# Block products over twenty k tiles of the second FFN projection, with the weights' block sums formed in HBM

## The chip, the cores and the metric

The kernel runs on one core of a Trainium2 chip. The metric is device time in microseconds (us) of one execution. The engines are PE (TensorE, matrix products), DVE (VectorE), ACT (ScalarE), POOL (GpSimd) and SP (SyncE), which here only issues DMAs. Each engine runs its own queue of instructions in order and waits at the head of it on semaphores. DMAs are issued on SP's, ACT's or POOL's queue and are carried out by 16 DMA engines.

## The reference, cut to what matters

One decoder block on x (512 tokens by 1024 channels), fp32. The part that changes is the end of it:

```
h2 = rms_norm(x, norm2_g) * (1 + scale2) + shift2
f_g, f_u = split(h2 @ w_ffn_in)            # w_ffn_in: 1024 x 5632, so two halves of 2816
x = x + gate2 * ((silu(f_g) * f_u) @ w_ffn_out)   # w_ffn_out: 2816 x 1024
return rms_norm(x, final_norm_g)
```

2816 is 22 k tiles of 128 rows. The second FFN projection is therefore a product of 512 tokens, 22 k tiles and 1024 columns.

## The kernel before, in words

Every fp32 product is done in three matmuls. Each operand is split into a rounded high part (an ACT copy to fp32r) and the low rest (a DVE subtraction), and `mm3` (lines 51 to 55) issues high by high, high by low and low by high into the same PSUM bank. A matmul takes 128 rows of k, 128 tokens and up to 512 columns.

The program is written in the order in which it runs on each engine; the semaphores follow from the tiles that the instructions read and write. The buffers are named by tags, and a tag with one buffer is handed on when the last reader of its old tile is done.

Weights come through a stream (lines 58 to 148). `issue` starts the DMA of a chunk of 128 x 1024 elements, 512 KB, into one of three `raw` buffers; `prep` makes its high and low parts in one of three `hi` and three `lo` buffers; `get(i)` makes sure that everything up to two chunks behind chunk i has been prepared and that as many more have been issued as `raw` buffers allow.

The first FFN projection (from line 1620) runs in 20 rounds, q = -2 to 17. A round computes 256 columns of f_g or f_u for all tokens by seven block products (Strassen and Winograd's scheme over halves of tokens, k and columns) of 12 matmuls of 256 columns each. `s_issue(q + 2)` at the head of a round issues two loads of 512 KB on SP's queue; `s_prep(q + 1)` spreads the splits and sums of the next round's weights over the round. In rounds 1 to 8 the last adaLN section is accumulated too (`last_mod`, line 1452 on). The results are the tiles `gq`, 22 of them with 512 tokens each, made by `gtile`.

The second FFN projection follows (lines 1716 to 1859). k tiles 12 to 19 (`KZ`) are done by seven block products, `zprod`, over halves of the tokens (256), of these k tiles (4) and of the columns (512). The sums of activations (`a_sum`) and the differences of weights (`w_sub`) are made by DVE in place, and their splits by `a_hi`, `a_lo`, `w_hi` and `w_lo`. The other 14 k tiles (`KC`) are done plainly, in seven chunks of two k tiles for each of the two column halves (`W_FO`), with the activations split by `g_split` into the tiles `gs`. Behind the first column half stand the residual additions for it (`resid`, line 1162: a product with the gate, an addition to x, and a square with a sum) and `scale_g`, which multiplies by the gain of the final norm. In the second half the last three chunks are done token tile by token tile, so that a row block can be normalised (`row_rstd`, `finish`) while the next one is computed. The last token tile is done in two parts of 256 columns.

The lines that set the two sets of k tiles are these:

```
KZ, KC = (list(range(12, 16)), list(range(16, 20))), list(range(12)) + [20, 21]
W_FO = [[add_w(w_ffn_out, KC[k:k + 2], 512 * h, 512) for k in range(0, len(KC), 2)] for h in range(2)]
```

Of the kernel before, what the change touches and what calls it, by code (L numbers as in the profile page):

```python
# [28 lines left out]
def block_kernel(ctx: ExitStack, tc: tile.TileContext, x, positions, w_ada, b_ada, w_in,  # L29
# [239 lines left out]
    KZ, KC = (list(range(12, 16)), list(range(16, 20))), list(range(12)) + [20, 21]  # L269
    W_FO = [[add_w(w_ffn_out, KC[k:k + 2], 512 * h, 512) for k in range(0, len(KC), 2)] for h in range(2)]  # L270
# [95 lines left out]
    def sec_tasks(flush=False, one=False):  # L366
        tick[0] += 1
        while sec_done:
# [31 lines left out]
    hT = [(base.tile([128, S], F32R, name=f"h{kt}", tag=f"S1_{kt}", bufs=1),  # L400
           base.tile([128, S], F32R, name=f"hl{kt}", tag=f"S1_{8 + kt}", bufs=1)) for kt in range(8)]
# [682 lines left out]
    mT, om, ow, oraw = {}, {}, {}, {}  # L1084
    OM = {"A11": 0, "S1": 1, "S2": 2, "A12": 3, "S3": 0, "S4": 1, "A22": 2}
# [24 lines left out]
    def o_m(key):  # L1110
        om[key] = tuple(base.tile([128, 2, 256], F32R, name="om", tag=f"S1_{OM[key] + 8 * e}", bufs=1) for e in range(2))
        split(*om[key], m_block(key))
# [8 lines left out]
    def pb_evac(g):  # L1121
        def ev(pb):
            for m in range(2):
                k = 2 * g + m
                t, o = t512("mg"), part[k // 4][:, k % 4]
                V.tensor_mul(t, pb[m], gbt[g][:, m])
                V.tensor_add(o, o, t)
                if k >= 4:
                    mT[k] = tuple(base.tile([128, S], F32R, name="mt", tag=f"S1_{k + 8 * e}", bufs=1) for e in range(2))
                    A.activation(mT[k][0], o, AF.Copy)  # L1130
            for k in range(2 * g, 2 * g + 2):
                if k >= 4:
                    V.tensor_sub(mT[k][1], part[1][:, k % 4], f(mT[k][0]))
        return ev
# [27 lines left out]
    def resid(p, c0, n, slot, tk, gate):  # L1162
# [4 lines left out]
        A.activation(t[:, :n], xt[tk][:, cs_], AF.Square, scale=1.0 / 32, accum_out=ss2[:, tk, slot:slot + 1])  # L1167
# [19 lines left out]
    def norm2_T(half):  # L1187

        for kh in range(2):
# [5 lines left out]
            else:  # L1195
                h2f["t", kh, 1] = [base.tile([128, 2, 256], F32, name="h2f", tag=f"S1_{kh * 2 + q}", bufs=1)
                                   for q in range(2)]
# [20 lines left out]
    sraw, sw = {}, {}  # L1218
# [27 lines left out]
    def s_prep(q):  # L1246
# [4 lines left out]
        d = sw[q] = {}  # L1251
        A11, A21, A12, A22 = ra[:, :, 0], ra[:, :, 1], rb[:, :, 0], rb[:, :, 1]

        def a0():
            d["A"] = tuple(base.tile([128, 4, 128], F32R, name="sa", tag="acc", bufs=2) if q == -2 else
                           base.tile([128, 4, 128], F32R, name="sa", tag=f"S1_{4 + 2 * (q % 2) + e}", bufs=1)
                           for e in range(2))
# [149 lines left out]
    gq, gz = {}, []  # L1407

    def gtile(m):
        if m not in gq:  # L1410
            if m < 12:
                gq[m] = base.tile([128, S], F32, name="gq", tag=f"S1_{m + 8 if m < 8 else m - 8}", bufs=1)
            else:
                n = 4 if m < 20 else 2
                t = ffn[0].tile([128, n, S], F32, name="gq", tag=("E5", "E6", "F1")[(m - 12) // 4], bufs=1)
                for e in range(n):
                    gq[m + e] = t[:, e]
                gz.append(t)
# [46 lines left out]
    def last_gate():  # L1465
        t = ffn[0].tile([128, 4, S], F32R, name="ahl", tag="E6", bufs=1)
        for half in range(2):
# [6 lines left out]
    gT = {}  # L1474

    GHOME = ["E1", None, "E3", None, "E0", None, ("S1_4", "S1_5"), ("S1_6", "S1_7"), "S2_2", "S2_3", "E7", None,
             "S2_4", "S2_5"]
    spare = []

    def g_home(n):  # L1480
        h = GHOME[n]
        if h is None:
            return spare.pop()
        if isinstance(h, tuple):
            return [base.tile([128, S], F32R, name="gs", tag=t, bufs=1) for t in h]
        if h[0] == "S":
            t = base.tile([128, 2, S], F32R, name="gs", tag=h, bufs=1)
        else:
            t = ffn[0].tile([128, 4, S], F32R, name="gs", tag=h, bufs=1)
            spare.append((t[:, 2], t[:, 3]))  # L1490
        return t[:, 0], t[:, 1]

    def g_split(upto):
        while len(gT) < min(upto, len(KC)):
            m = KC[len(gT)]
            hi, lo = g_home(len(gT))
            split(hi, lo, gq[m])
            gT[m] = (hi, lo)


    zr, zw, za = {}, {}, {}
    ZW = {"T1": ("E2", "E4"), "T2": ("E1", "E3"), "T3": ("E0", "E7"), "T4": ("E2", "E4"), "B22": ("E1", "E3")}
    ZA = {"A11": 0, "S1": 4, "S2": 6, "A12": 0, "S3": 4, "S4": 6, "A22": 0}

    def z_issue(name):
        kh, h = {"B11": (0, 0), "B12": (0, 1), "B21": (1, 0), "B22": (1, 1)}[name]
        for c in range(2):
            if name == "B11" or name == "B12" and c == 0:
                t = base.tile([128, 2, S], F32, name="raw", tag="raw", bufs=RAWB)
                ts = [t]  # L1510
            elif name == "B12":
                ts = [ffn[0].tile([128, 2, S], F32, name="zraw", tag="F0", bufs=1)]
            elif name == "B22":
                ts = [base.tile([128, 2, S], F32, name="zraw", tag=f"S2_{2 + c}", bufs=1)]
            else:
                ts = [base.tile([128, 1, S], F32, name="zraw", tag=f"S1_{4 + 2 * c + e}", bufs=1) for e in range(2)]
            k = KZ[kh][2 * c]
            for t in ts:
                n = t.shape[1]
                SY.dma_start(t, w_ffn_out[k * 128:(k + n) * 128, h * 512:h * 512 + 512].rearrange("(j p) n -> p j n", p=128))  # L1520
                k += n
            zr[name, c] = ts

    def z_parts(ts, *others):
        o = 0
        for t in ts:
            n = t.shape[1]
            yield (t,) + tuple(x_[:, o:o + n] for x_ in others)
            o += n

    def w_hi(key, c, src):
        if key in ZW:
            t = ffn[0].tile([128, 2, 2, S], F32R, name="zw", tag=ZW[key][c], bufs=1)
            zw[key, c] = (t[:, 0], t[:, 1])
        else:
            zw[key, c] = tuple(base.tile([128, 2, S], F32R, name=n, tag=n, bufs=3) for n in ("hi", "lo"))
        for t, hi in z_parts(zr[src, c], zw[key, c][0]):
            A.activation(hi, t, AF.Copy)

    def w_lo(key, c, src):  # L1540
        for t, hi, lo in z_parts(zr[src, c], *zw[key, c]):
            V.tensor_sub(lo, t, f(hi))

    def w_sub(o, a, b, c):

        (o_,), (b_,) = zr[o, c], zr[b, c]
        for a_, ob, bb in z_parts(zr[a, c], o_, b_):
            V.tensor_sub(ob, a_, bb)

    def a_block(name):  # L1550
        kh, th = {"A11": (0, 0), "A21": (0, 1), "A12": (1, 0), "A22": (1, 1)}[name]
        return gz[kh][:, :, th * 256:(th + 1) * 256]


    AT_ = {"A11": "A11", "A12": "A12", "A22": "A22", "S1": "A21", "S4": "A21", "S2": "A11", "S3": "A11"}

    def a_hi(key):
# [344 lines left out]
```

## Time and profile before

| what | value |
|---|---|
| time, median of 3 runs | 829.84 us (829.57 to 829.93) |
| time of the profiled execution | 829.8 us |
| its span in the trace | 828.0 us |
| PE busy | 815.7 us, 99% |
| DVE busy | 672.2 us, 81% |
| ACT busy | 413.6 us, 50% |
| POOL busy | 108.5 us, 13% |
| bytes moved by DMA | 109.10 MB |
| granted PE clock | 0.998 |

Times inside the trace are counted from the start of the span. Busy times of matmuls overlap, since the array is pipelined: a row's mean duration is longer than the distance between two matmuls, and the distance is what counts for the time. DVE's and ACT's durations contain a short overlap of the same kind. A DMA's "landing" is the time from its issue to its completion.

### The profile page before, as it was taken

The numbers are of one execution on the slowest core, as the hardware profiler recorded it, in microseconds if no ns is written. First come the engines' busy times: TensorE is split into PE (matmuls) and PEld (weight loads), VectorE is DVE, ScalarE is ACT, GpSimd is POOL, SyncE is SP. The second block draws the span as 40 slices with busy tenths as digits, with TensorE's granted clock in tenths as the row PEclk, the third lists the DMA queues.
The fourth block names the chain that finished last, engine by engine and source line by source line (L and its number), as shares of the span: only waits on it lengthen the run. The fifth ranks groups of instructions, "written<-read, shape, count | busy, mean of one in ns | idle before, by whom it ended". The sixth has DMA issues, their size and how long they took to land.

```text
span 828.0 us, 12858 instructions
## 1 busy us (share of the span) xinstructions
PE 815.7 (99%) x4980; PEld 730.0 (88%) x4980; DVE 672.2 (81%) x1161; ACT 413.6 (50%) x722; POOL 108.5 (13%) x101
## 2 busy tenths in 40 slices
PE   7999999999999999999999999999999999999996
PEld 6889889988888888988888899999999999888885
DVE  7989788798899558886697969799998888984635
ACT  5674544323322236665536586555555555563322
POOL 2060032362353411000000000000000000000001
PEclk9999999999999999999999999999999999999999
DMA  9974352423445562057631403445533335143212
GB/s 299 311 201 118 102 178 78 121 85 101 124 136 180 195 181 74 26 158 231 197 102 47 157 27 128 124 152 159 168 111 103 103 102 155 50 153 102 77 51 103
DMA packets 95677, 109.10 MB, mean 132 GB/s; under 512 B 5616, under 2 KB 76272, under 8 KB 95616
## 3 DMA queue, kind: packets, MB, share of 16 engines
q1 hardware_dynamic: 92512, 101.37, 40.2%
q0 software_dynamic: 2384, 6.10, 2.3%
q8 instruction: 39, 0.64, 0.3%
q10 hardware_dynamic: 720, 0.82, 0.3%
q14 instruction: 22, 0.18, 0.1%
HBM read 105.90 MB, written 2.10 MB: 130 GB/s over the span
## 4 chain that ended last, share of the span: by engine, by line
PE 96%; DMA 1%; DVE 1%; issue 0%; SPq 0%; ACT 0%; POOLq 0%; POOL 0%; DVEq 0%
PE pb L55 9%; PE pb L53 9%; PE pb L54 9%; PE R L53 8%; PE R L54 8%; PE R L55 8%; PE pfo L55 5%; PE pfo L53 5%; PE pfo L54 5%; PE pav L54 2%; PE pav L53 2%; PE pav L55 2%; PE pgb L53 2%; PE pgb L54 2%; PE pgb L55 2%; PE po L54 2%
## 5 line engine op out<-in xcount | busy, mean ns | idle before, releaser
L112 ACT ACTIVATE hi<-raw 128x1024 fp32r<-128x1024 f32 (+2 forms) x80 | 82.5, 1034 | 105.4 <-PE pb L54 39.9
L116 POOL TENSOR_TENSOR lo<-raw,hi 128x1024 fp32r<-128x1024 f32 x29 | 73.0, 2522 | 127.8 <-ACT hi L112 122.1
L116 DVE TENSOR_TENSOR lo<-raw,hi 128x1024 fp32r<-128x1024 f32 (+2 forms) x44 | 53.0, 1210 | 41.4 <-ACT hi L112 41.2
L53 PE MATMUL pb<-h,hi 128*128 128x512 f32 (+1 forms) x192 | 74.6, 388 | 0.0
L55 PE MATMUL pb<-h,lo 128*128 128x512 f32 (+1 forms) x192 | 73.9, 385 | 0.0
L54 PE MATMUL pb<-hl,hi 128*128 128x512 f32 (+1 forms) x192 | 73.9, 385 | 0.0
L177 DVE SCALAR_TENSOR_TENSOR acc<-mraw,cols,acc 128x512 f32<-128x512 f32 x49 | 40.1, 818 | 17.9 <-DMA mraw<-in_w_ada_dram 16.9
L55 PE MATMUL pfo<-hi,gs 128*128 128x512 f32 (+1 forms) x126 | 46.4, 369 | 0.0
L54 PE MATMUL pfo<-lo,gs 128*128 128x512 f32 (+1 forms) x126 | 46.4, 368 | 0.0
L53 PE MATMUL pfo<-hi,gs 128*128 128x512 f32 (+1 forms) x126 | 46.4, 368 | 0.0
L53 PE MATMUL R<-tb,sx 128*128 128x256 f32 x160 | 45.2, 282 | 0.0
L54 PE MATMUL R<-tb,sx 128*128 128x256 f32 x160 | 45.1, 282 | 0.0
L55 PE MATMUL R<-tb,sx 128*128 128x256 f32 x160 | 45.0, 281 | 0.0
L55 PE MATMUL R<-tb,lo 128*128 128x256 f32 x160 | 44.8, 280 | 0.0
L53 PE MATMUL R<-tb,hi 128*128 128x256 f32 x160 | 44.8, 280 | 0.0
L54 PE MATMUL R<-tb,hi 128*128 128x256 f32 x160 | 44.6, 279 | 0.0
L55 PEld LDWEIGHTS pb<-h,lo 128*128 128x128 f32 x192 | 36.0, 187 | 7.3
L54 PEld LDWEIGHTS pb<-hl,hi 128*128 128x128 f32 x192 | 36.0, 188 | 6.9
L53 PEld LDWEIGHTS pb<-h,hi 128*128 128x128 f32 x192 | 36.0, 188 | 6.9
L54 PE MATMUL pav<-lo,h 128*128 128x256 f32 x128 | 35.8, 279 | 0.0
L53 PE MATMUL pav<-hi,h 128*128 128x256 f32 x128 | 35.7, 279 | 0.0
L55 PE MATMUL pav<-hi,hl 128*128 128x256 f32 x128 | 35.7, 279 | 0.0
(392 smaller groups left out, 2655.4 us busy)
## 6 DMA issues: line engine op xcount, KB each, us to landing
raw<-in_w_ffn_in_dram SPq DMA_DIRECT2D x44, 512.0 KB, 4.6
raw<-in_w_in_dram SPq DMA_DIRECT2D x40, 512.0 KB, 3.9
mraw<-in_w_ada_dram SPq DMA_DIRECT2D x28, 512.0 KB, 4.1
raw<-in_w_ffn_out_dram SPq DMA_DIRECT2D x17, 512.0 KB, 3.8
s<-in_w_ada_dram SPq DMA_DIRECT2D x30, 256.0 KB, 5.6
raw<-in_w_proj_a_dram SPq DMA_DIRECT2D x8, 512.0 KB, 4.8
raw<-in_w_proj_b_dram SPq DMA_DIRECT2D x8, 512.0 KB, 4.6
raw<-in_w_in_dram SPq DMA_DIRECT2D x9, 256.0 KB, 4.7
```

Of the source, the lines that this page charges most:

```text
L53: T.matmul(o, wh, rh, start=start, stop=False, **kw)
L54: T.matmul(o, wh, rlo, start=False, stop=False, **kw)
L55: T.matmul(o, wlo, rh, start=False, stop=stop, **kw)
L112: A.activation(hi[:, :m], e["raw"][:, :m], AF.Copy)
L116: e["lo"].tensor_sub(lo[:, :m], e["raw"][:, :m], f(hi[:, :m]))
L177: V.scalar_tensor_tensor(o, w, cs[:, j:j + 1], o, op0=OP.mult, op1=OP.add)
```

## The change

- `KZ` becomes 20 k tiles: ten for each half, the k tiles 0 to 19. A block product is then 5 chunks of two k tiles (`NZ = 5`) for 2 token tiles. Only k tiles 20 and 21 are left in `KC`, one chunk for each column half.
- The four sums of weight blocks that the scheme needs are no longer made by DVE from loaded blocks. Four tensors `wsum` of 1280 x 512 elements lie in HBM. `wsum_steps` fills them, in pieces of 256 rows (512 KB): a copy from HBM to HBM on SP's queue, and additions by accumulating DMAs on POOL's queue. With the halves of k and of columns as indices the sums are: 1 is B00 + B01, 3 is B01 + B11, 2 is 1 + B11, 4 is 2 + B10. For each of the five pieces this is four copies and four accumulating DMAs, in six steps. `wstep()` is called twice in each round of the first projection, and takes one step each time.
- Signs are turned so that only additions are needed in HBM: `z_copy` gets a factor of -1 and `z_add` an operation.
- All block operands of weights, those in HBM too, now come through the stream: `zprod` fetches its five chunks by `get` and between them runs a list of small tasks: `a_hi`, `a_lo`, `a_sum` for later products, and residual additions.
- The products are in another order: those that finish column half 0 and parts of half 1, then the plain chunks, then two block products (`"A22"` with sum 4, and `"S4"` with block (1, 1)), between whose chunks the residual additions stand. The three last chunks of the last product are done token tile by token tile.
- `S1` is summed in three parts, in rounds 9, 13 and 16. The 16 tags `S1_0` to `S1_15` of 128 x 512 become four tags `SW0` to `SW3` of 128 x 4 x 512, so that the `gq` tiles lie by fours.

```diff
-    KZ, KC = (list(range(12, 16)), list(range(16, 20))), list(range(12)) + [20, 21]
-    W_FO = [[add_w(w_ffn_out, KC[k:k + 2], 512 * h, 512) for k in range(0, len(KC), 2)] for h in range(2)]
+    KZ = ([0, 1, 2, 3, 4, 5, 6, 7, 12, 13], [8, 9, 10, 11, 16, 17, 18, 19, 14, 15])
+    KC = [20, 21]
+    NZ = 5
+    dram = ctx.enter_context(tc.tile_pool(name="dram", bufs=1, space=bass.MemoryType.DRAM))
+    wsum = {n: dram.tile([NZ * 256, 512], F32, name=f"wsum{n}") for n in (1, 2, 3, 4)}
+    W_Z = {}
...
+    for key in ((0, 0), 1, 2, (1, 0), 3):
+        add_z(key)
+    W_FO = [add_w(w_ffn_out, KC, 512 * h, 512) for h in range(2)]
+    for key in (4, (1, 1)):
+        add_z(key)
+    def wsum_steps():
+        def step(c, *moves):
+            o = slice(256 * c, 256 * c + 256)
+            def fn():
+                for n, add, src in moves:
+                    if isinstance(src, tuple):
+                        k = KZ[src[0]][2 * c] * 128
+                        src = w_ffn_out[k:k + 256, 512 * src[1]:512 * src[1] + 512]
+                    else:
+                        src = wsum[src][o]
+                    if add:
+                        P.dma_start(wsum[n][o], src, accum_op=OP.add)
+                    else:
+                        SY.dma_start(wsum[n][o], src)
+            return fn
+        parts = [[step(c, *m) for m in (
+            ((1, 0, (0, 0)), (3, 0, (0, 1))), ((1, 1, (0, 1)), (3, 1, (1, 1))), ((2, 0, 1),), ((2, 1, (1, 1)),),
+            ((4, 0, 2),), ((4, 1, (1, 0)),))] for c in range(NZ)]
+        return ([fn for c in (0, 2) for two in zip(parts[c], parts[c + 1]) for fn in two] +
+                [fn for one in parts[4] for fn in (one, None)])
...
+    def sw(k, dt, name):
+        return base.tile([128, 4, S], dt, name=name, tag=f"SW{k}", bufs=1)
...
     def z_first():
+        def b(k):
+            return lambda: ensure(wseq[wseq.index(W_Z[0, 0][0]) + k])
+        st["limit"] = 1 << 30
+        return [(b(0), lambda: a_hi("A11", 0), lambda: a_lo("A11", 0)),
+                (b(1), lambda: a_hi("A11", 1), lambda: a_lo("A11", 1)),
+                (lambda: a_hi("A11", 2), lambda: (a_lo("A11", 2), a_sum("S2", 0))),
+                (b(2), lambda: None)]
...
         sprod(R[1], S2_, TB[2], False)
+        wstep()
         A.activation(R[2], R[1], AF.Copy)
...
-        if q == NQ - 2:
-            a_sum("S1")
-    z_issue("B22")
+        wstep()
+        if q in (9, 13, NQ - 2):
+            a_sum("S1", {9: 0, 13: 2}.get(q, 1))
...
+    def zprod(k, ka, kw, start, tasks):
         if start:
             Z[k] = [bank(ZB[k][e], "pfo") for e in range(2)]
+        for c, i in enumerate(W_Z[kw][:len(tasks)]):
+            w = get(i)
+            for fn in tasks[c]:
+                fn()
             for e in range(2):
+                zmm(Z[k][e], ka, c, e, w, ALL, start and c == 0, c == NZ - 1)
...
+    z_copy(1, 0, -1.0)
+    zprod(3, "S1", 1, True, [[lo_("S2", 1), hi_("S2", 2), sm_("S4", 0), lo_("S2", 2)], [sm_("S4", 1), hi_("A12", 0)],
+                             [sm_("S4", 2), lo_("A12", 0)], [hi_("A12", 1)],
+                             [lo_("A12", 1), hi_("A12", 2)]])
...
+    zprod(2, "A22", 4, False, [[res_(0, 0)], [sq_, res_(1, 0)], [sq_, res_(2, 1)], [sq_, res_(3, 1)], [sq_]])
...
+    zprod(1, "S4", (1, 1), False, [[res_(2, 0)], [sq_, res_(3, 0)]])
+    last = bank(7, "pfo")
+    A.activation(last[:, :256], Z[1][1][:, 256:], AF.Copy)
+    ids = W_Z[1, 1][2:]
+    ch = [get(i, 2 - k) for k, i in enumerate(ids)]
+    sq_()
+    done(2)
+    done(3)
+    for tk in range(2):
+        for z in range(2) if tk else (None,):
+            c = ALL if z is None else slice(256 * z, 256 * z + 256)
+            o = Z[1][0] if z is None else (Z[1][1][:, :256], last[:, :256])[z]
+            for n_, w in enumerate(ch):
+                zmm(o, "S4", 2 + n_, tk, w, c, False, n_ == 2)
...
```

384 lines of the change are left out of this document (153 added, 231 removed).

## The prediction

> **What bounds the kernel now.** I read the page first: busy shares, then the chain that ended last.
>
> ```profile
> span 828.0 us, 12858 instructions
> PE 815.7 (99%) x4980; PEld 730.0 (88%) x4980; DVE 672.2 (81%) x1161; ACT 413.6 (50%) x722; POOL 108.5 (13%) x101
> ...
> PE 96%; DMA 1%; DVE 1%; issue 0%; SPq 0%; ACT 0%; POOLq 0%; POOL 0%; DVEq 0%
> ```
>
> The reader is to see 96% of the chain on PE. So matmuls that go away shorten the time, unless their place is taken by a wait. Next come the two stages that the change touches, by their tiles: `R` is the first FFN projection, `pfo` the second. The rows give durations, the first and last start, and the forms.
>
> ```profile
> L53 PE MATMUL R<-h,sa x80: 276/279/289, 503.8 to 695.0; 128*128 128x256 f32 x80
> L55 PE MATMUL R<-tb,sx x160: 277/283/283, 515.4 to 703.9; 128*128 128x256 f32 x160
> ...
> L53 PE MATMUL pfo<-hi,gs x126: 277/392/403, 743.0 to 820.6; 128*128 128x512 f32 x98, 128*128 128x256 f32 x28
> L53 PE MATMUL pfo<-zw,za x40: 389/394/400, 709.6 to 742.4; 128*128 128x512 f32 x40
> L53 PE MATMUL pfo<-hi,za x16: 392/396/400, 704.0 to 725.7; 128*128 128x512 f32 x16
> ...
> L55 PE MATMUL pfo<-hi,gs x126: 278/392/398, 743.5 to 820.8; 128*128 128x512 f32 x98, 128*128 128x256 f32 x28
> ```
>
> Each product is three such lines (L53, L54, L55). `R`: 20 rounds of 84 matmuls, 503.8 to 703.9, hence 0.119 us for 256 columns and 10.0 us a round. `pfo`: (98+40+16) x 3 = 462 matmuls of 512 columns and 28 x 3 = 84 of 256, from 704.0 to 820.8. With 84 x 0.119 = 10.0 us for the narrow ones, 462 share 106.8 us: 0.231 us each. Neither stage leaves PE idle, and the stages join without a gap.
>
> **The change part by part.** *Matmuls.* Before: 7 products x 4 k tiles x 2 token tiles x 3 = 168, and 14 x 4 x 2 x 3 = 336; in all 504 widths of 512. After: 7 x 10 x 2 x 3 = 420 and 2 x 4 x 2 x 3 = 48; in all 468. Only the last 18 widths are cut in two, so 450 wide and 36 narrow ones remain. Saved: 12 x 0.231 + 48 x 0.119 = 2.8 + 5.7 = **8.5 us**, all of it on the path.
>
> *DVE and ACT in the second projection.* A chunk now feeds 12 matmuls, 2.77 us, where a plain chunk fed 24. Its splits, and the distance of DVE operations of that size:
>
> ```profile
> L112 ACT ACTIVATE hi<-raw 128x1024 fp32r<-128x1024 f32 x14 | 14.7, 1058 | 39.2 <-PE pfo L55 35.3 <-DMA raw<-in_w_ffn_out_dram 3.8
> ...
> 724.73 1.21 DVE L1542 TENSOR_TENSOR zw<-raw,zw 128x1024 fp32r<-128x1024 f32 x1
> 725.86 1.21 DVE L1542 TENSOR_TENSOR zw<-zraw,zw 128x1024 fp32r<-128x1024 f32 x1
> ...
> 704.00:743.00 39.00, 39.00 (x170) 31.54 (x169) 35.86 (x42) 24.59 (x32) 0.53 (x1) 1.00 0.29 95
> ```
>
> DVE starts one every 1.13 us. A product lasts 60 x 0.231 = 13.9 us and asks DVE for five weight splits (5.7) and at most six operations on activations (6.8): 12.5 us at most, in the product with `S1`. ACT has five splits and at most about five other copies, some 10 us. DVE was busy 35.86 of 39 us while PE never paused, so I cost this at 0. The weight differences and the `gs` splits that go away were under PE too: also 0. `S1`'s sums in rounds 9 and 13 (1.13 and about 0.6 us) stand beside a PE that has 10 us of work a round; DVE has room there (third row of windows below): 0. The four wide tags are handed on at points where all readers of the old tile are a stage back: 0. By my reading the third chunk of the first product is asked for twice in round 17, by the stream's own rule and explicitly: 512 KB more under a full PE, 0.
>
> *Loads of the second projection.* 512 KB per 2.77 us is 189 GB/s.
>
> ```profile
> raw<-in_w_ffn_out_dram SPq DMA_DIRECT2D x17, 512.0 KB, 3.8
> raw<-in_w_ffn_in_dram SPq DMA_DIRECT2D x44, 512.0 KB, 4.6
> ...
> L1233 SPq DMA_DIRECT2D raw<-in_w_ffn_in_dram x40: 367/368/501, 460.0 to 674.0; - x40
> ...
> DMA to landing us min/median/max: 3.4/4.6/7.0
> ```
>
> With three `raw` buffers, one goes around in issue 0.4 + landing 3.8 + `hi` 1.06 + `lo` 1.21 = 6.5 us, and PE needs it every 8.3 us; prepared chunks are two ahead. I cost this at 0, with little room: landings of 5.6 us would use it up.
>
> *HBM sums in the first projection.* 20 copies on SP's queue and 20 accumulating DMAs on POOL's, 512 KB each, in rounds -2 to 15. POOL has no other work here, so what its DMAs wait for delays only them. SP's queue is shared: a copy of step 3 or 5 waits for accumulations of the step before, and behind it stand the next rounds' loads, for which ACT waits, and with it PE. The 16 engines' share and rate in the three stretches of six rounds:
>
> ```profile
> 507.00:566.00 59.00, 59.00 (x499) 59.00 (x499) 51.08 (x70) 33.42 (x60) 0.00 (x0) 1.00 0.45 138
> 566.00:625.00 59.00, 59.00 (x500) 59.00 (x499) 55.95 (x78) 34.41 (x62) 0.00 (x0) 1.00 0.46 141
> 625.00:684.00 59.00, 59.00 (x496) 58.82 (x496) 49.60 (x67) 33.62 (x60) 0.00 (x0) 1.00 0.34 101
> ...
> 561.67 12.55 SPq L1233 DMA_DIRECT2D raw<-in_w_ffn_in_dram  x4
> ...
> 574.85 0.62 ACT L1258 ACTIVATE sa<-raw 128x512 fp32r<-128x512 f32 x1
> ```
>
> 141 GB/s at 0.46 is 307 GB/s for all engines, so 512 KB costs 1.71 us of them. That is my price of a copy. No row shows an accumulating DMA. Bounds: below, a plain transfer's 1.71 us; above, the longest landing of 512 KB on POOL's queue, taken as if nothing overlapped:
>
> ```profile
> xr<-in_x_dram POOLq DMA_DIRECT2D x4, 512.0 KB, 4.3
> ...
> gate1b<-in_b_ada_dram POOLq DMA_DIRECT2D x1, 512.0 KB, 9.3
> ```
>
> I take 2.6 us: a copy reads and writes each byte once, an accumulation reads two operands and writes one, so three streams for two; landings contain a wait for completion that others can use, so the lower end is nearer. The first two stretches each take two of the five pieces: 0.45 x 59 = 27 us of loads, eight copies 13.7, eight accumulations 20.8, together 61 of 59 us. The third takes one piece: 20 + 6.8 + 10.4 = 37 us. What spills over is made good there. A load issued at 561.67 was first read at 574.85, 13.2 us later, and lands in 4.6: 8.6 us of slack. Dependent steps stand two rounds (20 us) apart in a stretch. So SP may stand for some microseconds without PE noticing, and the price is 0; if the slack is used up, every further microsecond is PE's.
>
> The Trainium skill, "DMA: Bandwidth & Descriptors", section "Issuing engines are not separate DMA queues", says that DMAs of all issuing engines run on the same 16 engines and interleave. By it the idle POOL gives no capacity of its own, as assumed above; without it the accumulations would cost nothing at any price. No run here shows either yet.
>
> *The tail.* In the last product DVE has chunk splits, two residuals (three operations of 128x512 each, 0.62 us apart) and two row ends, all on one queue:
>
> ```profile
> 744.08 1.29 DVE L306 TENSOR_TENSOR gs<-gq,gs 128x512 fp32r<-128x512 f32 x2
> ```
>
> Counting from that product's start: the split of its third chunk ends at 2.5 us (its `hi` buffer comes free at 0), residual 4.4, split 5.5, residual 7.4, split of the last chunk 8.5. PE wants that at 5.5 + 2.8 = 8.3: 0.3 us lost. The row ends and a third residual keep DVE until about 0.3 us after the last matmul's result. Before, DVE had idled 0.64 us when that result came:
>
> ```profile
> 821.14 0.42 DVE L1165 TENSOR_TENSOR rt<-pfo,gate2b 128x256 f32<-128x256 f32 x1 [0.64 <-PE pfo L55]
> ...
> 823.53 0.61 ACT L1708 ACTIVATE xo<-xo,sm 128x384 f32<-128x384 f32 x1 [0.96 <-POOL sm L1171]
> ```
>
> The 7 us from 821.14 to the span's end are the same work in both. Bounds of this term: 0 and, if a whole residual stands in front, 2; I take **+0.6**.
>
> Sum: 829.8 (span 828.0 and 1.8 around it) - 8.5 + 0.6 = **821.9 us**. The profiled execution is 0.04 us under the median 829.84, which changes nothing.
>
> **The rivals.**
>
> *The sums in HBM hold SP (slower).* Place: the copies of sums 2 and 4 on SP's queue, with the loads behind them. Over 177 us the engines have 74 us of loads (0.45, 0.46 and 0.34 of 59) and 34 of copies; the 20 accumulations, at a us each, fit with the 8.6 us of slack if 108 + 20 a < 185.6, so a < 3.9 us. At a = 4.3 the lost time, about 8 us, eats the gain. At 5 it is 21 us: 843; at 9.3 it would be 107 us: 929. For it speak the load share, already 0.46, and 9.3 in the row above; against it the 4.3 of the `xr` row, a landing with its fixed part.
>
> *The same, partly.* a between 3.9 and 4.2, or bursts in the first stretch alone: 1 to 7 us lost, 823 to 829.
>
> *Loads bound the second projection.* Its share of DMA was only 0.29, but landings rise with traffic (7.0 us at worst in the row above). At 6.2 us a buffer goes around in 8.9 us, 0.2 us per chunk too long: 35 x 0.2 = 7 us, so 829, and slower above that. Against it: nothing else loads then, and 3.8 us is the median of that same stage.
>
> The page cited above gives 341 GB/s for a 1 MB load, in its section "Measured". By that figure a rough estimate of the point at which the first rival eats the gain rises by a tenth or two; the trace shows 307 at these sizes, and I stay with that.
>
> **How the numbers follow.** Forecast 0.50; sums in HBM hold SP, slower 0.22; partly 0.16; loads bound the second projection 0.12. The likeliest case alone spans 820.8 (8.5 saved, 0.5 better at the tail) to 823.5 (2 us at the tail). The range must leave out no more than 2 in 10: 820.5 to 834, which takes in the two middle cases and the mild end of the first rival, and leaves out the rest of that. 0.2% (1.7 us) is about what a measurement can tell from no change. Faster: 0.50 + 0.15 + 0.04 = 0.69; same 0.01 + 0.03 = 0.04; slower 0.22 + 0.05 = 0.27.
>
> **What would show it.** Right: `pfo` rows with 450 wide and 36 narrow matmuls over some 108.5 us; `R` still over 200 us; SP waits at the HBM copies short; DMA share of the first two stretches near 1 at most. An accumulation's own cost shows in the packets and share of the software queue. Wrong by the first rival: ACT at `sa<-raw` waiting for `raw` and `R` longer than 200 us. Wrong by the last: `hi<-raw` in `pfo` waiting for DMA, and PE below 90% there. The tail term is read from the distance between the last matmul and DVE's `rt`.

## The result, and the profile after

| | before | after |
|---|---|---|
| time, median of 6 runs each | 829.88 us | 832.63 us (831.31 to 833.28) |
| ratio, 95% interval | | 1.003 (1.0017 to 1.0043) |
| span of the profiled execution | 828.0 us | 829.5 us |
| first projection (`R`), first start to last start | 200.1 us | 206.2 us |
| second projection (`pfo`), the same | 116.8 us | 109.6 us |
| last issue of ACT's queue ends, to the span's end | 3.5 us | 4.8 us |

The change makes the kernel slower by 0.3%, where 1% faster was forecast. The profiled execution after is the fastest of its runs, so its 1.5 us over before is less than the median's 2.75. It divides so: `R` starts 0.8 later (its start lies between 503.1 and 505.0 in all runs below, with sums and without, so that is no part of the change), `R` +6.1, `pfo` -7.2, and the end behind the last matmul +1.8.

The page after: span, busy shares, the DMA share in 40 slices, and the two queues that carry nearly all bytes (packets, MB, share of 16 engines).

```profile
span 829.5 us, 12872 instructions
PE 810.3 (98%) x4920; PEld 723.6 (87%) x4920; DVE 684.5 (83%) x1167; ACT 427.0 (51%) x730; POOL 126.7 (15%) x121
DMA  9974352423345652057531409899998863556533
q1 hardware_dynamic: 99872, 120.24, 45.7%
q0 software_dynamic: 7824, 16.59, 10.4%
```

The same two queues before:

```profile
q1 hardware_dynamic: 92512, 101.37, 40.2%
q0 software_dynamic: 2384, 6.10, 2.3%
```

DMA now stands at 8 and 9 tenths for eight slices (the 25th on, from 498 us), nearly all of them in the first projection, where before only its loads ran and it stood at 3 to 5. The 20 accumulations are the software queue's 10.49 MB more; they cost 8.1% of 829.5 us, 67 us of all 16 engines, **3.36 us each**. The copies are priced in the first experiment. Such a price is the time of the packets, added up and divided by 16. The share of DMA in the windows below reaches 1.28, so packets' times can overlap in an engine, and a price is not time in which nothing else moves.

The groups by tile: duration, first and last start, forms.

```profile
L53 PE MATMUL R<-h,sa x80: 276/281/289, 504.6 to 701.6; 128*128 128x256 f32 x80
L55 PE MATMUL R<-tb,sx x160: 277/282/283, 516.2 to 710.8; 128*128 128x256 f32 x160
...
L55 PE MATMUL pfo<-hi,za x146: 280/395/397, 711.4 to 820.5; 128*128 128x512 f32 x134, 128*128 128x256 f32 x12
L53 PE MATMUL pfo<-hi,gs x16: 395/396/397, 780.5 to 791.6; 128*128 128x512 f32 x16
```

(134 + 16) x 3 = 450 wide and 36 narrow matmuls, as counted; the second projection starts at 710.9, 6.9 us later than before. Where `R` lost its time is seen in windows of it (PE, PEld, DVE, ACT, POOL busy; granted clock; DMA share; GB/s):

```profile
563.80:583.80 20.00, 20.00 (x171) 20.00 (x171) 19.08 (x27) 10.70 (x19) 3.53 (x4) 1.00 1.01 279
583.80:603.80 20.00, 16.31 (x123) 15.61 (x122) 13.43 (x22) 8.03 (x16) 1.76 (x2) 0.91 0.94 247
...
593.00:595.00 2.00, 2.00 (x14) 2.00 (x13) 1.96 (x3) 0.00 (x0) 0.00 (x0) 0.63 1.28 449
595.00:597.00 2.00, 1.58 (x8) 1.28 (x7) 2.00 (x3) 1.27 (x3) 0.00 (x0) 0.52 1.06 438
```

There is one disturbed place. PE stands for 3.7 of the 20 us from 583.8, and behind its first pause the granted clock is 0.63 and 0.52 for two windows of 2 us, which costs some 0.37 x 2.0 + 0.48 x 1.58 = 1.5 us more. Together that is 5.2 of the 6.1 us; 0.3 of the rest is there without any sums too (first experiment), and 0.6 I can't assign.

Who waits at this place (us in total, times, longest), and the landing of the 40 loads of the first projection:

```profile
DVE acc L175 <- DMA mraw<-in_w_ada_dram: 6.4, 1, 6.4
...
ACT sx L1335 <- DMA raw<-in_w_ffn_in_dram: 3.1, 1, 3.1
...
ACT sa L1324 <- DMA raw<-in_w_ffn_in_dram: 2.1, 1, 2.1
PE R L53 <- ACT R L1670: 2.1, 1, 2.1
```

```profile
DMA to landing us min/median/max: 3.4/6.6/16.1
```

ACT and DVE wait for loads, and PE for ACT. A load of the projection landed after 16.1 us at worst, 7.0 before. In the prediction's rows a load is first read 13.2 us after its issue (4.6 of landing and 8.6 of slack), so 16.1 us is 2.9 too late, and ACT's longest wait for a load is 3.1. What was in the engines is told by the view of DMA from 572 to 584 us, first after, then before:

```profile
q0 software_dynamic: 595, 1.16, 60.3%
q1 hardware_dynamic: 1088, 1.41, 37.8%
```

```profile
q1 hardware_dynamic: 1919, 2.42, 65.8%
```

Four accumulations were issued in these 12 us (572.97, 574.58, 575.88 and 577.18). They took 60.3% of the engines' time, and the loads, together with the last of the copies, got 37.8%, where 65.8% had been the loads': 1088 packets for 1919. That is how the loss in `R` comes about, as far as this trace shows it.

Four accumulations alone are not enough: the first four, issued at 506.75 to 510.74, stopped PE nowhere. The next loads were issued behind them, at 512.79 and after, and landed in 11.3 and 12.2 us, while two loads were issued in the midst of the later four (from 573.48). Nor did SP stand at its copies: its waits name no copy anywhere in this trace, and 71.0 and 50.6 us, the longest of the first projection, are for DVE to free the buffers of the loads.

SP's issues slowed, though: the loads' line and the copies' line have issues of 2.90 and 3.04 us, where 0.37 and 0.52 are usual.

```profile
L1298 SPq DMA_DIRECT2D raw<-in_w_ffn_in_dram x40: 367/368/2903, 460.5 to 680.5; - x40
...
L307 SPq DMA_DIRECT2D wsum<-wsum x10: 473/522/3041, 524.9 to 671.0; - x10
```

### The profile page after: what moved, and what is told of

Its sections match the earlier page's. It is cut to its first block, busy times and chain, and to the rows that moved or that the text cites. A ratio compares the mean times of both kernels' runs of the same rounds, so it can differ in the third digit from the quotient of the medians.

```text
span 829.5 us, 12872 instructions
## 1 busy us (share of the span) xinstructions
PE 810.3 (98%) x4920; PEld 723.6 (87%) x4920; DVE 684.5 (83%) x1167; ACT 427.0 (51%) x730; POOL 126.7 (15%) x121
## 3 DMA queue, kind: packets, MB, share of 16 engines
q1 hardware_dynamic: 99872, 120.24, 45.7%
## 4 chain that ended last, share of the span: by engine, by line
PE 50%; DVE 18%; DMA 6%; ACT 2%; issue 2%; POOL 0%; POOLq 0%; ACTq 0%; DVEq 0%
PE R L53 6%; PE R L54 6%; PE R L55 6%; DMA mraw<-in_w_ada_dram 6%; PE pfo L55 3%; PE pfo L53 3%; PE pfo L54 3%; DVE acc L177 3%; DVE sco L713 2%; DVE m L709 2%; PE pb L53 2%; PE pb L55 2%; PE pb L54 2%; DVE lo L116 2%; PE po L54 2%
## 5 line engine op out<-in xcount | busy, mean ns | idle before, releaser
L112 ACT ACTIVATE hi<-raw 128x1024 fp32r<-128x1024 f32 (+2 forms) x103 | 107.0, 1040 | 105.3 <-PE pfo L55 34.3
L116 DVE TENSOR_TENSOR lo<-raw,hi 128x1024 fp32r<-128x1024 f32 (+2 forms) x67 | 81.1, 1214 | 29.1 <-ACT hi L112 28.9
L53 PE MATMUL pb<-h,hi 128*128 128x512 f32 (+1 forms) x192 | 74.6, 389 | 0.0
L54 PE MATMUL pb<-h,hi 128*128 128x512 f32 (+1 forms) x192 | 74.0, 385 | 0.0
L54 PE MATMUL pfo<-lo,za 128*128 128x512 f32 (+1 forms) x146 | 56.3, 385 | 0.3 <-DVE lo L116 0.3
L55 PE MATMUL pfo<-hi,za 128*128 128x512 f32 (+1 forms) x146 | 56.2, 385 | 0.0
L53 PE MATMUL pfo<-hi,za 128*128 128x512 f32 (+1 forms) x146 | 56.1, 385 | 0.0
L305 POOL DMA_DIRECT2D wsum<-in_w_ffn_out_dram x20 | 17.8, 908 | 172.7 <-DMA wsum<-wsum 115.3
L54 PEld LDWEIGHTS pb<-h,hi 128*128 128x128 f32 x192 | 36.0, 188 | 6.9
L53 PEld LDWEIGHTS pb<-h,hi 128*128 128x128 f32 x192 | 36.0, 188 | 6.9
L1235 POOL TENSOR_TENSOR sm<-sm,mhalf 128x1 f32<-128x1 f32 x8 | 5.3, 662 | 217.6 <-DVE sm L1234 217.6
```

What stands on the lines that cost most here:

```text
L53: T.matmul(o, wh, rh, start=start, stop=False, **kw)
L54: T.matmul(o, wh, rlo, start=False, stop=False, **kw)
L55: T.matmul(o, wlo, rh, start=False, stop=stop, **kw)
L112: A.activation(hi[:, :m], e["raw"][:, :m], AF.Copy)
L116: e["lo"].tensor_sub(lo[:, :m], e["raw"][:, :m], f(hi[:, :m]))
L305: P.dma_start(wsum[n][o], src, accum_op=OP.add)
```

## The experiments

Theory 1: the moves of the sums and the loads share 16 engines, these are full in the first projection, and the loads come late. Theory 2, the prediction's first rival taken literally: SP stands at a copy, waiting for the moves before it, and the loads behind it are issued late. Ratios are to the kernel before on the same chip, with 95% intervals. The trace above already speaks against theory 2, since SP waits at no copy in it. Theory 1 doesn't stand as it is either: by the runs below it isn't the total of the moves that decides, but how close together they come.

**Without the sums.**

```
-                src, k0, c0 = wsum[key], 2 * c, 0
+                src, k0, c0 = w_ffn_out, KZ[0][2 * c], 0
...
-    wsteps = wsum_steps()
+    wsteps = []
```

> The sums in HBM are left out: the products with sums read block (0, 0) instead, so the output is not the reference's; everything else of the change stays. Theory 1 (the 16 DMA engines are full in the first projection, and loads come late) and theory 2 (SP's queue stands at the dependent copies, or loads lie behind copies in its ring) both expect the first projection to go back from 206.2 to 200.1 us and PE's idle time there to vanish: about 825 us. A third theory, that the lost time is not the sums' doing, expects 831 to 833. If the 1.3 us by which the end behind the last DMA issue grew belongs to the sums too, 824.

823.58 us, ratio 0.9932 (0.9915 to 0.9948). The groups by tile:

```profile
L55 PE MATMUL R<-tb,sx x160: 277/283/283, 514.7 to 703.5; 128*128 128x256 f32 x160
...
L55 PE MATMUL pfo<-hi,za x146: 280/395/398, 704.1 to 813.2; 128*128 128x512 f32 x134, 128*128 128x256 f32 x12
```

The page, its two queues:

```profile
q1 hardware_dynamic: 96832, 109.76, 42.5%
q0 software_dynamic: 2384, 6.10, 2.2%
```

`R` runs from 503.1 to 703.5, 200.4 us, and `pfo` 109.6 as in the changed kernel. So the saving of matmuls is real, and the sums take it away again: 0.98% between the two ratios, some 8 us. The copies' price follows too: 45.7% of 829.5 us against 42.5% of 821.0 is 30 us for 20 of them, 1.5 us each, where 1.71 was forecast.

**All the moves, hardly any bytes.**

```
-            o = slice(256 * c, 256 * c + 256)
+            o = slice(256 * c, 256 * c + 2)
...
-                        src = w_ffn_out[k:k + 256, 512 * src[1]:512 * src[1] + 512]
+                        src = w_ffn_out[k:k + 2, 512 * src[1]:512 * src[1] + 512]
```

> All 20 copies and 20 accumulations of the sums stay, with their places, their queues and their order, but each moves 2 rows (4 KB) and not 256 (512 KB). Left out: 254 of 256 rows of every sum; and the products with sums read rows of the first block of the weights, as in the run without sums, so the outputs are not the reference's. If what costs is the bytes in the engines at once: R as in the run without sums, 200.0 to 201.0 us, no stop of PE in 583 to 604, landings of the first projection's loads at most 8 us. If it were the waits of SP for the moves before: R stays above 202 us, since the chains of moves are the same. The distance from the end of ScalarE's last issue to the span's end: 4.6 to 5.0 us if it comes from the program (its instructions or where they lie), 3.4 to 3.8 if it comes from the bytes between places in HBM. Time: 823.5 to 825.0 us; by SP's waits 829 and more.

825.18 us, ratio 0.9938 (0.9921 to 0.9954); landings of the first projection's loads 6.6 us at worst. In the rows by tile below (then the last issue, and the instruction queue between 820 and 823.1 us) `R` runs from 504.0 to 704.3, 200.3 us:

```profile
L53 PE MATMUL R<-h,sa x80: 276/279/289, 504.0 to 695.2; 128*128 128x256 f32 x80
L55 PE MATMUL R<-tb,sx x160: 277/283/283, 515.5 to 704.3; 128*128 128x256 f32 x160
```

```profile
817.87 0.34 ACTq L1717 DMA_DIRECT2D out_dram<-xo  x1
...
q14 instruction: 1, 0.01, 1.0%
```

Same instructions, same order, same queues: the loss in `R` is gone. So it isn't the issuing of the moves. The run can't part bytes from waits, since a move of 4 KB lands in 2.5 us in the median and waits shrink with the bytes; the waits of SP are ruled out by the trace after the change. The end is another matter: 817.87 + 0.34 to 823.1 is 4.9 us, as long as after the change, so this part of the loss does not come from bytes.

**The copies on POOL's queue.** SP then issues no move at all.

```
-                        SY.dma_start(wsum[n][o], src)
+                        P.dma_start(wsum[n][o], src)
```

> The 20 copies from HBM to HBM are issued on POOL's queue, too, so SP issues loads alone and never waits for a sum. Theory 1: the same bytes go through the same engines, and now nothing holds them back, so the first projection is no shorter than 205 us: 830 or more. Theory 2: it takes 200 to 201 us: 825.

836.38 us, ratio 1.0088 (1.0066 to 1.0111): worse than the change itself. `R` takes 216.5 us. Windows of 20 us, and the landings of its loads:

```profile
544.00:564.00 20.00, 15.65 (x119) 15.18 (x117) 13.08 (x20) 6.94 (x13) 4.26 (x6) 0.91 1.08 276
564.00:584.00 20.00, 15.67 (x107) 15.47 (x108) 13.22 (x19) 7.63 (x14) 3.18 (x5) 0.83 1.06 327
...
DMA to landing us min/median/max: 3.3/7.1/25.0
```

Theory 2 falls. With SP free of the copies, PE stands for over 4 us in each of two windows, and not in one. What had spread the moves out was the place of the copies on SP's queue, behind loads that wait for their buffers. On one queue of its own the chain of moves is denser: its first and last issues lie at 486.7 and 628.9 us, where they lay at 497.8 and 677.3. This agrees with the section of the Trainium skill that the prediction cites ("Issuing engines are not separate DMA queues"): an idle issuer adds no capacity.

**Plain copies in place of accumulations.**

```
-                        P.dma_start(wsum[n][o], src, accum_op=OP.add)
+                        P.dma_start(wsum[n][o], src)
```

> Each accumulating DMA becomes a plain one of the same size on the same queue (it overwrites, so the sums are wrong); waits and order stay. Theory 1: the trace of after gives an accumulation 3.36 us of all engines and a copy 1.28; 20 x 2.1 = 42 us of engine time go away, the engines are no longer full, and the first projection takes under 201 us: about 825 to 826. Theory 2: the waits between the queues are all there, so 204 us or more and 830 or more.

826.01 us, ratio 0.9959 (0.9944 to 0.9973); `R` 201.4 us; loads land after 11.7 us at worst.

```profile
q0 software_dynamic: 5264, 16.59, 6.4%
```

The same bytes as after the change cost 4.2% of 825 us beyond the 2.2% of the queue's other work (run without sums), so 34.7 us or 1.73 us each: half of an accumulation's 3.36. At that price PE still loses 0.6 us at the same place. So an accumulation costs the engines as much as two plain transfers, and this doubling is most of the loss in `R`: nearly 5 of the 6.1 us go with it, though the bytes and the order of the moves stay.

**Without the adaLN loads beside it.** Is it the section's own loads, which come in the same rounds, that tip the place over?

```
-        if k % 2 == 0:
+        if k == 0:
...
-                mgl[k + e][0](mgr[e])
+                if k == 0:
+                    mgl[k + e][0](mgr[e])
```

> The changed kernel, with the six later loads of adaLN weights in rounds 3 to 7 left out (the first pair's tile is used again, so gate2 is wrong); the sums in HBM stay. 3.1 MB less in the stretch where PE stood: theory 1 expects no stop at 584 to 604, the first projection at 200.1 to 202 us and 826 to 827. If the dependent copies on SP's queue are what holds the loads, the stop stays: 831 or more.

831.78 us, ratio 1.0016 (1.0005 to 1.0027). The stop stays, with PE waiting 3.8 us in one piece:

```profile
584.00:604.00 20.00, 16.24 (x117) 16.04 (x116) 13.81 (x22) 7.94 (x16) 1.76 (x2) 0.83 0.83 204
```

They don't, and what theory 1 expected (no stop) is refuted. The other outcome, 831 or more, had been written down for SP's copies holding the loads; but SP waits only 0.7 us at a copy in this run. The share of 0.83 belongs to the 20 us of the stop, behind which little moves; in the 20 us ahead of it the share is 1.00. From 572 to 584 us the accumulations take 61.2% of the engines' time, as much as after the change. So the stop comes with the burst of the sums' moves, with or without the section's loads: here too, two loads are issued in its midst, at 573.09 and after, and loads land after 17.8 us at worst.

**Another timetable.** The first four pieces begin in the stages before, by position (the list names piece and step).

```
+    WAT = {("s", 0): "00", ("s", 1): "10", ("s", 6): "01", ("s", 7): "11", ("s", 10): "02", ("s", 11): "12",
+           "f": "20 30 03 13", (-2, 0): "21", (-1, 0): "31", (0, 0): "04", (0, 1): "14", (1, 0): "22", (2, 0): "32",
...
+    def wstep(at):
+        for cs in WAT.pop(at, "").split():
+            wsteps[int(cs[0])][int(cs[1])]()
```

> The same moves, in another timetable: the first two pieces start in the attention stage, where DMA is nearly idle, two others at the end of the stage before the first projection, and rounds 1 to 8, which load adaLN weights too, get one step each at most. Theory 1: no stretch of 20 us has its engines full for long; the first projection takes 200 to 202 us and the time is 825 to 827. Theory 2: SP still waits for each dependent copy; little better than 831.

827.51 us, ratio 0.9971 (0.9952 to 0.9989); its runs lie between 824.2 and 829.96. `R` 201.4 us, PE waits 0.5 in it. The DMA share is 1.00 in the first 20 us and 0.58 in those from 564, where the stop had been. Why its runs scatter so is not shown.

**One move at a time.** The same 40 moves in the same rounds, but the two of a step parted, so that at most two accumulations follow each other.

```
-            ((1, 0, (0, 0)), (3, 0, (0, 1))), ((1, 1, (0, 1)), (3, 1, (1, 1))), ((2, 0, 1),), ((2, 1, (1, 1)),),
-            ((4, 0, 2),), ((4, 1, (1, 0)),))] for c in range(NZ)]
+            ((1, 0, (0, 0)),), ((1, 1, (0, 1)),), ((2, 0, 1),), ((2, 1, (1, 1)),),
+            ((4, 0, 2),), ((4, 1, (1, 0)),), ((3, 0, (0, 1)),), ((3, 1, (1, 1)),))] for c in range(NZ)]
```

> The changed kernel, all sums still formed in its 20 rounds on the same queues, 20 copies and 20 accumulations, but one move in each of the 40 places: the copy and the accumulation of sum 3 of each piece stand behind those of sum 4, so that two accumulations follow each other where four did. The engines' total work is that of the changed kernel. If the total decides (loads, copies and accumulations over the length of the stage, as the prediction had it), the first projection again takes 204 to 206 us and the time is 831 to 833. If it is the burst of four accumulations beside loads (about 13 us of all engines at one time, more than the 8.6 us of slack of a load), the first projection takes 200 to 202 us and the time is 825 to 827.

828.93 us, ratio 0.9985 (0.997 to 0.9999), runs from 826.38 to 833.16 (the profiled one took 831.17). In `R` (201.7 us) the loss is nearly gone, with the same bytes: two pauses of 0.3 us, no drop of the clock, landings of 11.2 us at worst.

```profile
564.00:584.00 20.00, 20.00 (x171) 20.00 (x170) 19.08 (x27) 10.70 (x19) 1.76 (x2) 1.00 0.90 244
584.00:604.00 20.00, 19.67 (x166) 19.47 (x166) 18.22 (x26) 11.19 (x20) 1.76 (x2) 1.00 0.90 254
```

So it is how densely the moves come and not their total. The expected length of `R` came out, the expected time (825 to 827) didn't: the moves now take all rounds, and the last of them run on into the second projection, which takes 114.4 us. Its waits, and the issues at its start:

```profile
ACT hi L112 <- DMA raw<-wsum: 13.6, 6, 6.3
ACT hi L112 <- DMA raw<-in_w_ffn_out_dram: 7.7, 3, 5.9
...
PE pfo L54 <- DVE lo L116: 2.8, 5, 1.0
```

```profile
702.06 0.61 SPq L307 DMA_DIRECT2D wsum<-in_w_ffn_out_dram  x1
...
712.68 0.88 POOL L305 DMA_DIRECT2D wsum<-in_w_ffn_out_dram  x1 [13.66 <-DVE gq L1682]
```

The copy at 702.06 comes 4 us ahead of the second projection, the accumulation at 712.68 lies in it. And here SP does stand at a copy: 7.5 us up to the one issued at 693.54, with the next loads of weights behind it. Whether that wait or the traffic makes those loads late is not parted by any run. The loss is moved, not removed.

**Narrower accumulations.** Each as two DMAs of 256 columns, hence rows of 1 KB and not 2.

```
-                        P.dma_start(wsum[n][o], src, accum_op=OP.add)
+                        for e in range(2):
+                            ce = slice(256 * e, 256 * e + 256)
+                            P.dma_start(wsum[n][o, ce], src[:, ce], accum_op=OP.add)
```

> The changed kernel with every accumulating DMA cut into two of 256 columns each, so with rows (and packets) of 1 KB instead of 2 KB; timetable and bytes are the same. In the trace of the changed kernel a packet of an accumulation takes 198 ns of its engine and one of a load 53. If the engines take turns packet by packet, a load beside accumulations gets 53/(53+198) = 0.21 of them, and with packets half as long 53/(53+99) = 0.35: the worst landing of a load falls from 16 to about 10 us, the stop of PE gets much shorter, and the time is 826 to 829. If the bytes in the burst alone matter, or the cost of a packet does not shrink with it, it is 831 or more.

827.16 us, ratio 0.9961 (0.9949 to 0.9973); `R` 200.9 us and no pause of PE in it. The software queue, and the landing of the first projection's loads:

```profile
q0 software_dynamic: 13264, 16.59, 11.1%
...
DMA to landing us min/median/max: 3.5/6.8/13.9
```

And the window in which the changed kernel had its stop:

```profile
584.00:604.00 20.00, 20.00 (x169) 19.82 (x169) 18.04 (x26) 10.69 (x19) 3.37 (x4) 1.00 1.12 306
```

The accumulations got dearer, 3.66 us per 512 KB ((11.1 - 2.2)% of 823.6 us for 20), and the kernel got faster: a packet of them takes 108 ns in place of 198, the loads land after 13.9 us at worst in place of 16.1, and the accumulations after 22.1 in place of 14.9. PE works through at a share of 1.12, fuller than the 1.01 and 0.94 around its stop in the changed kernel. So how full the engines are doesn't decide alone; whose packets they carry does too. This run is also the plainest case against theory 2, for SP stands at copies here, and `R` is short all the same:

```profile
SPq L309 <- DMA wsum<-in_w_ffn_out_dram: 15.5, 4, 5.5
```

Whether the shorter packets help by themselves, or because the accumulations take longer and leave room, is not shown. The Trainium skill, "DMA: Bandwidth & Descriptors", section "Queues, rings and completion order", says that an engine goes round its rings and changes between them only at packet boundaries. The direction of this run agrees with it; its size doesn't confirm it, for turns packet by packet were to bring the worst landing to about 10 us, and 13.9 is measured.

**The moves where DMA is idle.** As the timetable above, with the moves in three gaps of the profile before the first projection, and the rest one by one.

```
+    WAT = {("s", 0): "00", ("s", 1): "10", ("s", 6): "01", ("s", 7): "11", "o": "02 12 20 03 13 21",
+           "w": "04 14 22 30", "f": "05 15 23 31", (-1, 0): "24", (-1, 1): "32", (1, 0): "25", (2, 0): "33",
+           (4, 0): "34", (6, 0): "35", (9, 0): "40", (11, 0): "41", (12, 1): "42", (13, 1): "43", (14, 1): "44",
+           (15, 1): "45"}
```

> The same 40 moves, in a timetable made from the stretches in which the trace of before shows a DMA share near 0 (330 to 350, 425 to 450, 470 to 490 us): three pieces are nearly done before the first projection, whose rounds get 7 copies and 7 accumulations instead of 20 and 20. Theory 1 (full engines): no stretch of 20 us in the first projection above a share of 0.8, no idle PE there, 200.1 to 200.6 us for it; 824 to 825, and less scatter than the 824.2 to 830.0 of the run before. Theory 2 (SP's waits) expects no better than that run, 827.

825.49 us, ratio 0.9945 (0.9932 to 0.9957). `R` takes 200.3 us at shares of 0.48 to 0.77 and PE waits nowhere in it; `pfo` takes 109.6. All 10.49 MB of accumulations are still made.

**The tail, first try.** On top of that the split of two chunks of the last product on POOL, and the split of `gs` earlier.

```
-            W_Z[key].append(add_w(src, [k0, k0 + 1], c0, 512))
+            W_Z[key].append(add_w(src, [k0, k0 + 1], c0, 512, P if key == (1, 1) and c in (1, 3) else None))
...
+    zprod(2, "S3", 3, False, [[hi_("S4", 0), g_hi], [lo_("S4", 0), hi_("S4", 1)], [lo_("S4", 1), g_lo, hi_("S4", 2)],
+                              [lo_("S4", 2)], [load_fng]])
```

> As the run before, and two changes at the end: the low parts of the second and the fourth chunk of the last product are made on POOL (2.5 us each, beside DVE), and the split of the last two k tiles' activations stands two chunks earlier. If DVE's backlog costs the second projection its 1.4 us over 108.3 us, it now takes 108.4 us, DVE's last work starts 0.3 us after the last matmul, and the time is 1.0 to 1.5 us below the run before: 823. If POOL's slower split is late instead, PE waits for it at the fourth chunk and nothing is won.

827.80 us, ratio 0.9974 (0.9965 to 0.9983): 2.3 us slower than without it. The same edit on the kernel without sums:

> The kernel without sums in HBM (products with sums read block (0, 0) instead, so the output is not the reference's) and with the two changes at the end. This is what the matmuls alone save: 823.6 less 1.0 to 1.5 us, so 822.1 to 822.6; the second projection takes 108.4 us. If DVE's backlog is not the reason for its 1.4 us, it stays 823.6.

825.45 us, ratio 0.9948 (0.9933 to 0.9964), against 0.9932: slower too, so it isn't the sums. In both PE waits 1.4 us for `lo` and 1.0 us for `hi` in `pfo`, as the second outcome had it; the wait for `gs` is gone. A split takes POOL 2.52 us, twice as long as DVE (1.21, in the prediction's rows). The group in the kernel without sums:

```profile
L116 POOL TENSOR_TENSOR lo<-raw,hi 128x1024 fp32r<-128x1024 f32 x31 | 78.1, 2523 | 224.5 <-ACT hi L112 218.8
```

**The tail, second try.** The gaps' timetable, the earlier `gs` split, the chunks' splits back on DVE, and the products with the final gain on POOL.

```
+    def scale_g(c0, n, tk, eng=V):
...
+        eng.tensor_mul(xo[tk][:, cs_], xt[tk][:, cs_], fng[0][:, cs_])
...
+            scale_g(512 * h, 512, tk, P)
```

> The kernel with the timetable in the gaps (825.5), with the split of the last two k tiles' activations two chunks earlier and the gain products of six residuals on POOL instead of DVE (3.7 us less on DVE in the last two products, 1.2 to 1.5 us each on POOL, beside it). If DVE's backlog is what costs the second projection its 1.3 us over 108.3, it now takes 108.4 to 108.8 us and the time is 0.7 to 1.3 us lower: 824.2 to 824.8. If POOL and DVE disturb each other or the row ends wait for POOL, it is 825.5 or more.

824.61 us (824.39 to 826.01), ratio 0.9935 (0.9923 to 0.9947). This is the fastest version with the reference's result: 5.6 us faster than before on its chip. `R` takes 200.4 us, `pfo` 108.6, and no wait of PE is left in `pfo`:

```profile
L55 PE MATMUL R<-tb,sx x160: 277/283/283, 516.0 to 704.8; 128*128 128x256 f32 x160
...
L55 PE MATMUL pfo<-hi,za x146: 278/395/397, 705.4 to 813.5; 128*128 128x512 f32 x134, 128*128 128x256 f32 x12
```

## Why the prediction was wrong, step by step

*Matmuls, -8.5.* Right. Both counts came out, and 450 x 0.231 + 36 x 0.119 = 108.2 us stands against 108.6 where nothing else disturbs (the second try at the tail) and 109.6 after the change.

*DVE and ACT in the second projection, 0.* Wrong by 0.55 us, half of what lies between these two. The split of `gs` comes late in the product with `S3`, and PE waits for it. The working had checked the product with `S1` and had called the `gs` splits that go away covered, without checking the one that stays. What a wait costs is read from the distances of the starts: 780.74, 781.42 and 781.75 are 1.01 us for two matmuls that take 0.46 elsewhere. The other half is at the split of the last chunk (next term). From the timeline after:

```profile
780.74 0.40 PE L54 MATMUL pfo<-lo,gs 128*128 128x512 f32 x1
781.42 0.50 PE L55 MATMUL pfo<-hi,gs 128*128 128x512 f32 x1 [0.28 <-DVE gs L1782]
...
814.44 0.40 PE L53 MATMUL pfo<-hi,za 128*128 128x512 f32 x1
815.13 0.50 PE L54 MATMUL pfo<-lo,za 128*128 128x512 f32 x1 [0.29 <-DVE lo L116]
...
821.11 0.42 DVE L1225 TENSOR_TENSOR rt<-pfo,gate2b 128x256 f32<-128x256 f32 x1
...
824.31 0.35 ACTq L1717 DMA_DIRECT2D out_dram<-xo  x1
```

*The tail, +0.6.* Nearly right as far as DVE goes. PE's wait for the split of the last chunk is 0.29 us in the trace (0.3 forecast), but by the distances (814.44, 815.13, and the next start at 815.46) it cost 0.56. DVE's `rt` starts 0.57 us behind the last matmul at 820.54, where it was 0.31 (821.14 behind 820.83). Together that is 0.8. What was left out is the end of the program: "the same work in both" it was, but from the last issue's end it takes 4.8 us and not 3.5.

*Loads of the second projection, 0.* Right; the rival "Loads bound the second projection" fell. `raw<-wsum` lands in 3.7 us in the median, and ACT's `hi` waits 1.1 us for loads in all. Loads came late enough to stop PE there only in the run with one move at a time, where moves were still under way.

*HBM sums in the first projection, 0.* Here the prediction failed, twice in one term, and the second is what decides. First the size: 2.6 us was taken for an accumulation and 3.36 is measured, inside the bounds of 1.71 and 9.3. But by the prediction's own inequality, 108 + 20 a < 185.6, that is still under 3.9 and should have cost nothing. So the step that failed is the inequality itself, and with it the sentence "What spills over is made good there." It compares totals over six rounds and over the whole stage with the engines' time. But a load must land before it is read, some 13 us after its issue, not within the stage: it can be late by its slack of 8.6 us and no more. Four accumulations in a row are 4 x 3.36 = 13.4 us of all engines; from 572 to 584 us the loads and the last copies together got 37.8% of the engines' time, and a load that takes 16.1 us can't be made good later. The runs show it from three sides: the same bytes one at a time (stop nearly gone), the same bytes in shorter packets (gone), the same burst without the adaLN loads (stop stays). (A small slip: at 5 us an accumulation the inequality gives 22 us lost, not 21.)

*The first rival* had the right place of loss, ACT and PE behind late loads, but a wrong mechanism in "hold SP": SP waited at no copy in the changed kernel, and with the copies taken off its queue the time got worse. "The same, partly" named bursts and 1 to 7 us; that is the case that came nearest, in the second stretch rather than the first. Its 823 to 829 was too low, since neither the `gs` split nor the longer end was in it.

The profiled execution after, 831.31 us, is 9.4 over the forecast: `R` 6.1, the end 1.4, the later start of `R` 0.8, the `gs` split 0.55, the tail 0.2 beyond its 0.6, and `pfo`'s matmuls 0.2, together 9.25.

## What to carry to other kernels

Transfers that are hidden by their total aren't hidden by their burst: compare the longest run of back-to-back transfers, in time of all engines, with the slack of the load that shares the engines, and place such work in the gaps that the DMA slices show. The comparison is a warning, not a law: 13.4 us against 8.6 stopped PE where loads were issued in the midst of the burst, and didn't where they came behind it, nor, at 14.6 us, with shorter packets. Price an accumulating DMA as two plain ones until measured (3.36 and 1.73 us here). And when an operation is moved off a busy engine, the target's duration for it counts against the time until its reader, not against the target's idle share.

## What was not expected of the hardware

*The clock can fall after a short stop.* PE stood for 2.1 us before 592.18 (`R <- ACT R` in the waits), and from 593 to 597 the granted clock was 0.63 and 0.52. It was 0.91 and 0.83 over the 20 us of the long stops in the run with copies on POOL, and stayed 1.00 in the windows where PE paused for 0.3 us (one move at a time). It isn't the length of the stop alone: after the waits of 1.0 and 1.4 us in the tail's first try the clock was 0.70 and 0.50 (810 to 814 us), and after the same waits in the kernel without sums it stayed 1.00. A pause of some microseconds can cost a good deal more than itself. The Trainium skill, "TensorE: Matmul & The Clock Gate", section "What's actually happening", puts the fall to half rate behind an idle window of about 3.4 us; here it followed a stop shorter than that.

*An issue can take 2 us and more.* Single issues on SP's queue took 2.90 and 3.04 us where 0.37 and 0.52 are usual; while one lasts, SP issues nothing else.

*The end of the program depends on the program.* From the end of ACT's last issue to the span's end it takes 3.5 us before, 3.6 with the copies on POOL, 3.7 without sums (with the tail's edit too), and 4.8 or 4.9 after and in the runs with SP's copies (4.5 and 4.6 with the edits of the tail, 3.9 with narrow accumulations). With two rows per move it is 4.9, so it doesn't come from bytes. The long ends are found only with the twenty copies in SP's program, but the narrow accumulations have these too and end in 3.9, so the copies don't settle it. In several of the long ones a load of instructions lies in the last 3 us, as in the row of that run; after the change, between 827.5 and 828.5 us, it is this:

```profile
q14 instruction: 1, 0.01, 3.1%
```

There is none in the last 3 us of before or of the run without sums, but none either in some of the long ones. That such a load is the cause is not shown; it stays open.
